# A hybrid decoder block with a top-4-of-32 expert layer: row sums moved into the routing, filler products on TensorE, and a last pair with finer loads, reordered sums and a norm spread over three engines

## The chip, the cores and the metric

The kernel runs on one core of one Trainium2 chip. The metric is the device time of one execution in microseconds (us); of several executions of a kernel the median counts. TensorE is called PE (its weight loads PEld), VectorE DVE, ScalarE ACT, GpSimd POOL, and the queue of SyncE that issues the loads SPq.

## What is computed

One decoder block for 256 tokens of 1024 channels: two token mixers (mLSTM and retention) merged by gates, and then the part that takes three quarters of the time, a layer of 32 experts of which each token uses four. Cut to what matters here:

```python
x = x + gate_m * mixer(h, ...)                       # 256 x 1024
h = rmsnorm(x, norm_ffn_g) * (1.0 + scale_f) + shift_f
logits = h @ w_router + b_router                     # 256 x 32
top_val, top_idx = lax.top_k(logits, 4); top_w = softmax(top_val)
gu = xb @ w_gate_up[e] + b_gate_up[e]                # per expert: 1024 x 2048
y  = clamped_swiglu(gu) @ w_down[e] + b_down[e]      # per expert: 1024 x 1024
x = x + gate_f * sum over the four experts of top_w * y
return rmsnorm(x, norm_final_g)
```

All weights are float32: 12.6 MB for an expert, 403 MB for the 32.

## The kernel before

**Routing.** After the output projection `wout` of the mixer, the residual `x` is transposed (`x1T`), multiplied with the router's weights (`logits`), normalised by one factor per token (`rc`, from a square root on ACT at L63), and the four largest logits give the mask. Three small products (`pos`) number each expert's tokens. The vector `gf` (the gate of the layer, 1024 values) is kept as partial sums on 128 partitions; `row_sum` (L219, L220) makes a row of it that stands on every partition by a product with `ones` and a copy on ACT. Its two halves are summed in pair 0, in the blocks n = 1 and 2.

**Pairs.** Two experts form a pair; there are 16 pairs, one after the other, each with 64 token slots for either expert. For a pair, `gather` builds a 0/1 matrix `oh` and multiplies it with `x` (`xgp`, L1115, eight 128-column products to a `step`); ACT and DVE scale the result into `xg`. Then come six blocks of products: four of `gup` (L1239, gate and up, n = 0 to 3) and two of `dnp` (L1277, down). Each block starts with two small bias products (L224) and runs k = 0 to 7 over the weights of the block, which come as two tiles `a` (k below 4) and `b` of 2 MB each. A product in float32 stands as two records in the profile, so a tile's eight products are "x16". After a `gup` block DVE and ACT make the clamped SwiGLU, and PE transposes it (`aTp`) into `aT`. After a `dnp` block DVE weights the result with the slot's weight and `gf` (`yp`, L1284), ACT and DVE split it in a high and a low part (`yph`, `ypl`), and four products `ya` (L1300) add it to the tokens' sums `yacc`.

**Order.** From the last part of `wout` on, PE runs its instructions in the order in which the code is written. Small work that belongs to the block just finished (the transposes, `ya`) is put in a list `waiting`, and `fill()` empties it within the products of the next block, after k = 4 of a `gup` and k = 3 of a `dnp`. SPq issues every load in the order of the code; a load waits until its buffer's former products are done, and until the eighth load before it has landed.

**The last pair (pair 15).** Its last block is cut into pieces of 256, 128 and 128 columns (`TAIL`), whose weights come in eight loads of 0.5 MB (`taila`, `tailb`). Here `ya` of the block before is not left to the next block: a `fill()` stands right behind it. Each piece is weighted (`yp`) and multiplied back to the tokens (`y`, L1290) at once. `finish` is called for four column ranges, `FIN = (0, 512, 768, 896)`. For each it adds the result to the residual (L1166), squares and sums it (L1168), multiplies by the final norm's row `gn` (L1172), all on DVE. After the last range, the sum gives the norm's factor, ACT and DVE scale the output (L1183 to L1185) and SPq stores it:

```python
                yp = tmp.tile([128, 512], F32, name=f"yp{pair}{n}{c0}", tag="yp", bufs=1)[:, :c1 - c0]
                dve.scalar_tensor_tensor(yp, p[:, :c1 - c0], wsl, gf[:, cs], op0=OP.mult, op1=OP.mult)
                if todo:
                    finish(*todo.pop())
```

Of the kernel before, what the change touches and what calls it, by code (L numbers as in the profile page):

```python
# [10 lines left out]
F32 = mybir.dt.float32  # L11
# [9 lines left out]
D = 1024  # L21
# [91 lines left out]
def block(ctx, tc, I, out, dbg=None):  # L113
# [11 lines left out]
    def f32v(ap):  # L125
        return ap.bitcast(F32)
# [100 lines left out]
    with ExitStack() as mctx:  # L227
# [768 lines left out]
        part = 0  # L996
        for z in range(2):
            w = wslot(wb(z), f"wout{z}", dim=1 + z)
            for c0, c1 in ((0, 256), (256, 512)) if z else ((0, 512),):
# [13 lines left out]
                for i in range(0, 2 * nk, 4):  # L1013
                    tk = [(j // nk, k0 + j % nk) for j in range(i, i + 4)]
                    p = tr(f"x1T{part}{i}")
                    for j, (t, k) in enumerate(tk):
                        pe.transpose(p[:, j * 128:(j + 1) * 128], x[:, t, k * 128:(k + 1) * 128], ident)
                    xt = sb(m2, [128, 4, 128], f"xt{part}{i}", tag="x1T", bufs=2)
                    act.activation(xt.rearrange("p k j -> p (k j)"), p, AF.Copy)
                    for j, (t, k) in enumerate(tk):  # L1020
                        pe.matmul(lp[:, t * E:(t + 1) * E], xt[:, j], wrs[:, k],
                                  start=k == 0 and t == 0, stop=k == 7, skip_group_check=True)
                if part == 1:
                    act.activation(warm, ss[:, 0, 0:1], AF.Sqrt)
                    dve.tensor_add(ss[:, 0], ss[:, 0], ss[:, 1])
# [24 lines left out]
        pe.matmul(pp[:, E:2 * E], tri[:, 1], mask[:, 0], start=False, stop=True)  # L1050

# [106 lines left out]
    o, todo = [], []  # L1158

    def finish(base, c0, c1, src):  # L1160
# [6 lines left out]
        for t in range(2):  # L1167
            dve.scalar_tensor_tensor(o[t][:, cs], x2[:, t, cs], 1.0, x2[:, t, cs], op0=OP.mult, op1=OP.mult,  # L1168
                                     accum_out=ss[:, i, t:t + 1])
        if c1 < D:  # L1170
            for t in range(2):
                dve.tensor_mul(o[t][:, cs], x2[:, t, cs], gn[:, cs])  # L1172
            if i:
                dve.tensor_add(ss[:, 0], ss[:, 0], ss[:, i])
            else:
                act.activation(ss[:, 4, 0:1], ss[:, 0, 0:1], AF.Sqrt)
            return
# [15 lines left out]
    def block_of(src, name):  # L1193
        tiles = [home(f"{name}{h}") for h in "ab"]
        for h in range(2):
            sp.dma_start(tiles[h], src[h])
        return Pairs(tiles)
# [4 lines left out]
    def dn(pair, n):  # L1202
        return block_of(I["w2"][pair, n], f"dn{pair}{n}")
# [4 lines left out]
    def fill():  # L1208

        while waiting:  # L1210
            waiting.pop(0)()
# [5 lines left out]
    for pair in range(NP):  # L1217
# [14 lines left out]
        for n in range(4):  # L1232
# [4 lines left out]
            for k in range(8):  # L1237
# [5 lines left out]
                if k == 4:  # L1243
                    fill()
                    if pair == 0 and n in (1, 2):
                        row_sum(gf, n - 1)
# [12 lines left out]
        for n in range(2):  # L1259
# [10 lines left out]
            for c0, c1 in cuts:  # L1270
# [12 lines left out]
                yp = tmp.tile([128, 512], F32, name=f"yp{pair}{n}{c0}", tag="yp", bufs=1)[:, :c1 - c0]  # L1283
                dve.scalar_tensor_tensor(yp, p[:, :c1 - c0], wsl, gf[:, cs], op0=OP.mult, op1=OP.mult)  # L1284
                if todo:
                    finish(*todo.pop())
                if last and n:
                    y2 = tr(f"y2{c0}").rearrange("p (t c) -> p t c", t=2)
                    for t in range(2):
                        pe.matmul(y2[:, t, :c1 - c0], f32v(ohT[:, t * 128:(t + 1) * 128]), yp, start=True, stop=True)  # L1290
                    todo.append((x2, 512 + c0, 512 + c1, [y2[:, t, :c1 - c0] for t in range(2)]))
                    continue
# [11 lines left out]
                if last:  # L1304
                    fill()
                    todo.append((x, 0, 512, [yacc[t][0] for t in range(2)]))
# [6 lines left out]
    finish(*todo.pop())  # L1313
# [161 lines left out]
```

## Time and profile before

| | |
|---|---|
| median of 3 runs | 1254.34 us (1252.33 to 1255.28) |
| the profiled execution's own time | 1252.83 us |
| its span, first to last instruction | 1251.0 us (1.83 us lie around it) |
| PE busy | 1172.1 us (94%) |
| DVE, ACT, POOL busy | 490.9, 289.4, 3.9 us |
| loaded from HBM | 476.46 MB, mean 382 GB/s |
| mean granted TensorE clock | 0.992 of full speed |

The profile is of one execution. "Busy" counts instructions that run; a busy PE need not be at its peak. The chain that ended last is followed back from the last instruction, at each step to what released it. Where the profile is asked for stretches, a row gives the stretch, its length, the busy time (and count) of PE, PEld, DVE, ACT and POOL, the granted TensorE clock as a share of full speed (1.00 is 2.4 GHz, 0.50 is 1.2 GHz), the share of time in which the 16 DMA engines moved data (it can read a little over 1), and the GB/s moved.

### The profile page before, as it was taken

To read this page: it belongs to the slowest core of one execution; us is meant where nothing else is said; L and a number is where in the kernel's file an instruction comes from. 1 tells how busy PE (TensorE), PEld (TensorE's weight loads), DVE (VectorE), ACT (ScalarE), POOL (GpSimd) and SP (SyncE) were. 2 spreads that over 40 slices of the span, in tenths; PEclk is the share of its full clock that TensorE was granted. 3 is DMA by queue.
4 is the path that set the end of the run, shared out by engine and by line. 5 is a ranking of instruction groups with operands and counts; after the bars stand their busy time and mean duration, and the time that the engine had idled before them with its cause. 6 is when DMAs were issued, how large, how long until landed. Compare 5 with 4: busy or idle time off the path is not lost.

```text
span 1251.0 us, 14561 instructions
## 1 busy us (share of the span) xinstructions
PE 1172.1 (94%) x5872; PEld 582.7 (47%) x5873; DVE 490.9 (39%) x1167; ACT 289.4 (23%) x559; POOL 3.9 (0%) x14
## 2 busy tenths in 40 slices
PE   8999999999899999999998989898989898998985
PEld 6878888888534334343342324232333333232423
DVE  5599889878322222221222222121213122222124
ACT  4585555565211111111110101010101101010111
POOL 0000000000000000000000000000000000000000
PEclk9999999999899999999999999999999999999998
DMA  9956779948899999999999999999999999999993
GB/s 362 366 184 212 292 275 359 353 185 333 318 425 428 427 428 426 429 426 428 427 428 427 427 427 429 428 426 427 428 429 427 427 427 427 430 427 427 427 422 117
DMA packets 43518, 479.12 MB, mean 383 GB/s; under 512 B 5554, under 2 KB 6514, under 8 KB 12212
## 3 DMA queue, kind: packets, MB, share of 16 engines
q1 hardware_dynamic: 42580, 477.53, 92.2%
q8 instruction: 48, 0.79, 0.3%
q10 hardware_dynamic: 864, 0.59, 0.2%
q14 instruction: 26, 0.21, 0.0%
HBM read 476.46 MB, written 1.05 MB: 382 GB/s over the span
## 4 chain that ended last, share of the span: by engine, by line
DMA 54%; PE 42%; DVE 2%; ACT 1%; issue 0%; SPq 0%; ACTq 0%; DVEq 0%
PE gup L1239 10%; PE dnp L1277 5%; DMA gu142b<-in_w 3%; DMA gu102b<-in_w 3%; DMA gu62b<-in_w 3%; DMA gu90b<-in_w 3%; DMA gu130b<-in_w 3%; DMA dn150b<-in_w 3%; DMA gu110b<-in_w 3%; DMA dn90b<-in_w 3%; DMA gu150b<-in_w 3%; DMA dn130b<-in_w 3%; DMA gu82b<-in_w 3%; DMA gu70b<-in_w 3%; DMA dn50b<-in_w 3%; DMA gu122b<-in_w 3%
## 5 line engine op out<-in xcount | busy, mean ns | idle before, releaser
L1151 DVE TENSOR_SCALAR g<-gup 128x256 f32<-128x256 f32 x64 | 27.2, 425 | 345.9 <-PE gup L1239 345.9
L1228 ACT ACTIVATE aT<-aTp 128x256 f32<-128x256 f32 x64 | 24.6, 384 | 286.1 <-PE aTp L1227 286.1
L1115 PEld LDWEIGHTS xgp<-oh,x 128*128 128x128 f32 x512 | 63.5, 195 | 51.4 <-issue 26.0
L1152 ACT ACTIVATE sg<-g 128x256 f32<-128x256 f32 x64 | 26.6, 416 | 255.0 <-DVE g L1151 251.9
L1121 DVE TENSOR_SCALAR xg<-xgp,fsc,fsh 128x128 f32<-128x128 f32 x64 | 26.2, 409 | 146.0 <-ACT xg L1123 146.0
L1115 PE MATMUL xgp<-oh,x 128*128 128x128 f32 x512 | 75.6, 292 | 1.0 <-DVE oh L1107 1.0
L1284 DVE SCALAR_TENSOR_TENSOR yp<-dnp,wsl,gf 128x512 f32<-128x512 f32 (+2 forms) x34 | 24.5, 720 | 114.7 <-PE dnp L1277 112.9
L1123 ACT ACTIVATE xg<-xgp,fsh,fsc 128x128 f32<-128x128 f32 x64 | 29.0, 454 | 153.5 <-PE xgp L1115 153.5
L1294 ACT ACTIVATE yph<-yp 128x512 fp32r<-128x512 f32 x31 | 19.5, 630 | 94.3 <-DVE yp L1284 94.3
L1227 PEld LDWEIGHTS aTp<-ca,a 128*128 128x128 f32 x128 | 13.7, 142 | 39.4 <-issue 39.4
L1155 DVE TENSOR_TENSOR a<-a,sg 128x256 f32<-128x256 f32 x64 | 27.2, 425 | 7.5 <-ACT sg L1152 1.0
L1300 PE MATMUL ya<-yph,ohT 128*128 128x512 f32 x62 | 27.8, 449 | 1.5 <-ACT yph L1294 1.5
L1154 DVE SCALAR_TENSOR_TENSOR a<-a,g 128x256 f32<-128x256 f32 x64 | 27.2, 425 | 2.1
L1227 PE MATMUL aTp<-ca,a 128*128 128x128 f32 x128 | 27.4, 296 | 0.0
L1153 DVE TENSOR_SCALAR a<-gup 128x256 f32<-128x256 f32 x64 | 26.6, 416 | 0.0
L1141 DVE TENSOR_SCALAR ohT<-cwp 128x256 fp32r<-128x256 f32 x16 | 6.8, 425 | 49.3 <-PE cwp L1140 49.3
L1295 DVE TENSOR_TENSOR ypl<-yp,yph 128x512 fp32r<-128x512 f32 x31 | 21.4, 689 | 11.9 <-ACT yph L1294 11.9
L224 PE MATMUL gup<-bex,id 96*64 96x512 bf16 x128 | 25.3, 390 | 0.0
L1300 PE MATMUL ya<-ypl,ohT 128*128 128x512 f32 x62 | 24.5, 396 | 0.2 <-DVE ypl L1295 0.2
L1300 PEld LDWEIGHTS ya<-yph,ohT 128*128 128x128 f32 x62 | 11.6, 187 | 28.1 <-issue 24.3
L224 PEld LDWEIGHTS <-id 96*64 96x64 bf16 x196 | 11.5, 109 | 25.7 <-issue 22.9
L1107 DVE TENSOR_SCALAR oh<-ca,posm,rc 128x64 f32<-128x64 f32 x64 | 17.0, 309 | 6.7 <-PE xgp L1115 6.7
(896 smaller groups left out, 2312.7 us busy)
## 6 DMA issues: line engine op xcount, KB each, us to landing
gu00a<-in_w SPq DMA_DIRECT2D x1, 2048.0 KB, 9.3
gu00b<-in_w SPq DMA_DIRECT2D x1, 2048.0 KB, 7.7
gu01a<-in_w SPq DMA_DIRECT2D x1, 2048.0 KB
gu01b<-in_w SPq DMA_DIRECT2D x1, 2048.0 KB, 7.7
gu02a<-in_w SPq DMA_DIRECT2D x1, 2048.0 KB
gu02b<-in_w SPq DMA_DIRECT2D x1, 2048.0 KB, 13.6
gu03a<-in_w SPq DMA_DIRECT2D x1, 2048.0 KB
gu03b<-in_w SPq DMA_DIRECT2D x1, 2048.0 KB
```

The lines of the kernel that those rows point to most:

```text
L224: pe.matmul(p[rows, :c1 - c0], id3[:, e:e + 1].to_broadcast([96, CAP]), bex[:, n, c0:c1], start=True, stop=False, skip_group_check=True)
L1115: pe.matmul(p[:, q * 128:(q + 1) * 128], x[:, t, k * 128:(k + 1) * 128], oh[:, t].rearrange("p q s -> p (q s)"), start=t == 0, stop=t == 1)
L1123: act.activation(xg[:, k], pq, AF.Identity, bias=fsh[:, k:k + 1], scale=fsc[:, k:k + 1])
L1151: dve.tensor_scalar(g[:r], v[:, 0], LIMIT, None, op0=OP.min)
L1152: act.activation(sg[:r], g[:r], AF.Sigmoid, scale=ALPHA)
L1153: dve.tensor_scalar(a[:r], v[:, 1], LIMIT, -LIMIT, op0=OP.min, op1=OP.max)
L1154: dve.scalar_tensor_tensor(a[:r], a[:r], 1.0, g[:r], op0=OP.add, op1=OP.mult)
L1155: dve.tensor_mul(a[:r], a[:r], sg[:r])
L1227: pe.transpose(p[:, q * 128:(q + 1) * 128], a[:, q * 128:(q + 1) * 128], ident)
L1239: pe.matmul(p[q * CAP:(q + 1) * CAP], xg[:, k, q * CAP:(q + 1) * CAP], w[q, k, slice(0, 512)], start=False, stop=k == 7, skip_group_check= ...
L1277: pe.matmul(p[q * CAP:(q + 1) * CAP, :c1 - c0], aT[:, k, q * CAP:(q + 1) * CAP], w[q, k, slice(c0, c1)], start=False, stop=k == 7, skip_gr ...
L1300: pe.matmul(yacc[t][n], ohT[:, t * 128:(t + 1) * 128], part, start=pair == i == 0, stop=i == 1 and pair >= NP - 2, skip_group_check=True)
```

## The change

There are four edits.

1. The row sums of `gf` leave pair 0. They are made in four quarters of 256 columns (`gate_sum`) in the routing: the first between the last transposes and the last `logits` products, three behind those `logits`. They take two PSUM buffers of the tag `mm`.
2. Five 128-column products of `ones` with itself (`idle`) stand behind the `pos` products. Nothing reads their result.
3. The two 2 MB loads `dn150a`, `dn150b` of the last pair's first `dnp` block become four of 1 MB, of two values of k each.
4. In the last pair, `ya` and the products `y` of each piece wait for the middle of the next piece's products, as elsewhere in the kernel. `finish` now squares and sums on ACT, except one of the two sums of the last range, and multiplies by `gn` on POOL for the first two ranges.

```diff
+        def gate_sum(i):
+            if i == 0:
+                gsum[:] = [mm(f"gsum{h}") for h in range(2)]
+            p = gsum[i // 2][:, i % 2 * 256:(i % 2 + 1) * 256]
+            pe.matmul(p, ones, gf[:, i * 256:(i + 1) * 256], start=True, stop=True)
+            act.activation(gf[:, i * 256:(i + 1) * 256], p, AF.Copy)
...
                     act.activation(xt.rearrange("p k j -> p (k j)"), p, AF.Copy)
+                    if part == 2:
+                        gate_sum(0)
                     for j, (t, k) in enumerate(tk):
                         pe.matmul(lp[:, t * E:(t + 1) * E], xt[:, j], wrs[:, k], ...)
+                if part == 2:
+                    for i in range(1, 4):
+                        gate_sum(i)
...
+        idle = tr("idle")
+        for _ in range(5):
+            pe.matmul(idle[:, :128], ones, ones, start=True, stop=True)
...
-        for t in range(2):
-            dve.scalar_tensor_tensor(o[t][:, cs], x2[:, t, cs], 1.0, x2[:, t, cs], op0=OP.mult, op1=OP.mult,
-                                     accum_out=ss[:, i, t:t + 1])
+        if c1 == D:
+            dve.scalar_tensor_tensor(o[0][:, cs], x2[:, 0, cs], 1.0, x2[:, 0, cs], op0=OP.mult, op1=OP.mult,
+                                     accum_out=ss[:, i, 0:1])
+        for t in range(c1 == D, 2):
+            act.activation(o[t][:, cs], x2[:, t, cs], AF.Square, accum_out=ss[:, i, t:t + 1])
         if c1 < D:
             for t in range(2):
-                dve.tensor_mul(o[t][:, cs], x2[:, t, cs], gn[:, cs])
+                (pool if c0 <= 512 else dve).tensor_mul(o[t][:, cs], x2[:, t, cs], gn[:, cs])
...
-    def block_of(src, name):
+    def block_of(src, name, step=2048):
         tiles = [home(f"{name}{h}") for h in "ab"]
         for h in range(2):
-            sp.dma_start(tiles[h], src[h])
+            for c in range(0, 2048, step):
+                cut = lambda ap: ap.rearrange("p (q c) -> p q c", q=2)[:, :, c:c + step] if step < 2048 else ap
+                sp.dma_start(cut(tiles[h]), cut(src[h]))
...
-        return block_of(I["w2"][pair, n], f"dn{pair}{n}")
+        return block_of(I["w2"][pair, n], f"dn{pair}{n}", 1024 if pair == NP - 1 else 2048)
...
                 if k == 4:
                     fill()
-                    if pair == 0 and n in (1, 2):
-                        row_sum(gf, n - 1)
...
-                if todo:
-                    finish(*todo.pop())
                 if last and n:
-                    y2 = tr(f"y2{c0}").rearrange("p (t c) -> p t c", t=2)
-                    for t in range(2):
-                        pe.matmul(y2[:, t, :c1 - c0], f32v(ohT[:, t * 128:(t + 1) * 128]), yp, start=True, stop=True)
-                    todo.append((x2, 512 + c0, 512 + c1, [y2[:, t, :c1 - c0] for t in range(2)]))
+                    def ended(c0, c1, yp, ohT):
+                        y2 = tr(f"y2{c0}").rearrange("p (t c) -> p t c", t=2)
+                        for t in range(2):
+                            pe.matmul(y2[:, t, :c1 - c0], f32v(ohT[:, t * 128:(t + 1) * 128]), yp, start=True, stop=True)
+                        finish(x2, 512 + c0, 512 + c1, [y2[:, t, :c1 - c0] for t in range(2)])
+                    waiting.append(lambda c0=c0, c1=c1, yp=yp, ohT=ohT: ended(c0, c1, yp, ohT))
                     continue
...
                 if last:
-                    fill()
-                    todo.append((x, 0, 512, [yacc[t][0] for t in range(2)]))
+                    waiting.append(lambda: finish(x, 0, 512, [yacc[t][0] for t in range(2)]))
...
-    finish(*todo.pop())
+    fill()
```

On PE in the last pair, from the end of the first `dnp` block on (`dnp` the product block, `ya` and `y` the products back to the tokens), it stood before:

```order
L1277 MATMUL dnp_6925<-dn150b,aT_6793 64x512 x8
L1300 MATMUL ya_2899<-yph_6950,ohT_6799 128x512
L1300 MATMUL ya_2899<-ypl_6951,ohT_6799 128x512
L1300 MATMUL ya_2901<-yph_6950,ohT_6799 128x512
L1300 MATMUL ya_2901<-ypl_6951,ohT_6799 128x512
...
L1277 MATMUL dnp_6968<-taila,aT_6793 64x256 x16
L1290 MATMUL y_6997<-yp_6987,ohT_6799 128x256 x2
...
L1277 MATMUL dnp_7000<-tailb,aT_6793 64x128 x16
L1290 MATMUL y_7028<-yp_7019,ohT_6799 128x128 x2
```

On PE at the same place of the changed kernel (whose line numbers differ):

```order
L1298 MATMUL dnp_6937<-dn150b,aT_6803 64x512 x8
...
L1298 MATMUL dnp_6976<-taila,aT_6803 64x256 x8
L1323 MATMUL ya_2915<-yph_6962,ohT_6809 128x512
L1323 MATMUL ya_2915<-ypl_6963,ohT_6809 128x512
L1323 MATMUL ya_2917<-yph_6962,ohT_6809 128x512
L1323 MATMUL ya_2917<-ypl_6963,ohT_6809 128x512
L1298 MATMUL dnp_6976<-taila,aT_6803 64x256 x8
...
L1298 MATMUL dnp_7009<-tailb,aT_6803 64x128 x8
L1311 MATMUL y_7020<-yp_7007,ohT_6809 128x256 x2
L1298 MATMUL dnp_7009<-tailb,aT_6803 64x128 x8
```

Each group of products back to the tokens now has half a block of products ahead of it that doesn't need it.

On DVE, the changed kernel's rows from the second piece on (`yp` the weighting, `end` the residual, `ss` the sums of squares, `o` and `end` also the output):

```order
L1305 SCALAR_TENSOR_TENSOR yp_7038<-dnp_7009,wsl_6810,gf 128x128
L1194 TENSOR_TENSOR ss<-ss 128x2
L1184 TENSOR_TENSOR end<-end,y_7051 128x128 x2
L1192 TENSOR_TENSOR o_6991<-end 128x128
L1192 TENSOR_TENSOR end<-end 128x128
L1194 TENSOR_TENSOR ss<-ss 128x2
L1305 SCALAR_TENSOR_TENSOR yp_7069<-dnp_7040,wsl_6810,gf 128x128
```

The last `yp` stands behind two products and a sum that wait for ACT's squares of the range before.

On ACT, the changed kernel's routing (`xt` the transposed residual, `gf` the copies of the row sums, `ss` the square root, `wm` the exponentials of the routing weights, `xg` the first gathered tokens):

```order
L1029 ACTIVATE xt_2847<-x1T_2842 128x512
L1005 ACTIVATE gf<-gsum_2849 128x256
L63 ACTIVATE ss<-ss 128x2
L1005 ACTIVATE gf<-gsum_2849 128x256
L1005 ACTIVATE gf<-gsum_2850 128x256
L1098 ACT_TABLE_LOAD
L1098 ACTIVATE wm<-lg,negm 128x32
L1005 ACTIVATE gf<-gsum_2850 128x256
L1098 ACTIVATE wm<-lg,negm 128x32
L1141 ACTIVATE xg_2924<-xgp_2925,fsh,fsc 128x128
```

Before, the square root followed `xt` at once, and the table load the square root; now one copy stands ahead of the square root, and two ahead of the table load.

## Rows read from the trace of the kernel before

**Rows 1.** stretches: engines' busy us (x instructions), PEclk, DMA share, GB/s

```profile
330.00:335.00 5.00, 5.00 (x30) 2.62 (x28) 0.51 (x2) 0.56 (x2) 0.00 (x0) 1.00 0.27 62
...
340.00:345.00 5.00, 4.53 (x20) 1.44 (x16) 2.06 (x7) 1.08 (x3) 0.00 (x0) 1.00 0.99 403
700.00:900.00 200.00, 184.78 (x878) 67.93 (x877) 47.89 (x124) 21.70 (x50) 0.00 (x0) 0.99 1.01 427
```

**Rows 2.** timeline of the load queue SPq: start us, us, what

```profile
319.11 0.42 SPq L1196 DMA_DIRECT2D dn01a<-in_w  x1
333.82 0.33 SPq L1196 DMA_DIRECT2D dn01b<-in_w  x1
```

**Rows 3.** who SPq waited for, 318 to 345 us: total, times, longest

```profile
SPq L1196 <- PE gup L1239: 21.7, 3, 14.2
```

**Rows 4.** chain that ended last, 324 to 376 us: start, us, what

```profile
324.52 3.75 PE xgp L1115 x16
328.27 0.57 PE gup L224 x2
...
330.82 1.09 PE xgp L1115 x8
331.91 1.87 PE gup L1239 x8
...
344.02 1.13 PE rs L219 x2
...
375.21 1.12 PE ya L1300 x4
```

**Rows 5.** timeline of PE: the first gather; [idle before <-releaser]

```profile
324.52 3.75 PE L1115 MATMUL xgp<-oh,x 128*128 128x128 f32 x16 [0.98 <-DVE oh L1107]
```

**Rows 6.** stretches of low PEclk, and the ones before them

```profile
319.00:322.60 3.60, 1.73 (x12) 1.25 (x12) 2.98 (x19) 2.08 (x3) 0.00 (x0) 0.97 0.94 328
322.60:329.10 6.50, 4.82 (x23) 4.09 (x24) 4.25 (x20) 1.45 (x4) 0.00 (x0) 0.50 1.01 431
...
1223.40:1226.90 3.50, 1.77 (x10) 0.95 (x10) 2.13 (x4) 1.91 (x2) 0.00 (x0) 1.00 0.59 241
1226.90:1230.10 3.20, 3.20 (x18) 1.85 (x16) 3.03 (x8) 0.20 (x1) 0.00 (x0) 0.51 0.20 81
```

**Rows 7.** timeline of PE and its weight loads, last pair

```profile
1214.74 3.65 PE L1277 MATMUL dnp<-dn150a,aT 128*64 128x512 f32 x16 [0.51 <-DMA dn150a<-in_w]
...
1219.79 3.65 PE L1277 MATMUL dnp<-dn150b,aT 128*64 128x512 f32 x16 [1.03 <-DMA dn150b<-in_w]
...
1230.31 1.25 PEld L1277 LDWEIGHTS dnp<-taila,aT 128*64 128x64 f32 x12 [0.19 <-issue]
...
1232.61 1.13 PE L1290 MATMUL y<-yp,ohT 128*128 128x256 f32 x4 [0.59 <-DVE yp L1284]
...
1236.21 0.71 PE L1290 MATMUL y<-yp,ohT 128*128 128x128 f32 x4 [0.54 <-DVE yp L1284]
```

**Rows 8.** chain that ended last, last pair: start us, us, what

```profile
1226.88 5.17 PE dnp L1277 x32
...
1237.10 1.78 PE dnp L1277 x32
...
1242.68 0.49 ACT o L1183
```

**Rows 9.** tile tailb: its four issues, and from issue to landing

```profile
L1267 SPq DMA_DIRECT2D tailb<-in_tail x4: 327/328/328, 1205.0 to 1219.7; - x4
...
DMA to landing us min/median/max: 10.0/13.7/17.3
```

**Rows 10.** groups by line: a GpSimd fill, a VectorE product, a ScalarE copy

```profile
L319 POOL MEMSET gf<- 128x1024 f32 x1 | 1.0, 956 | 0.0
...
L1172 DVE TENSOR_TENSOR o<-end 128x512 f32<-128x512 f32 x1 | 0.7, 684 | 0.0
...
L1228 ACT ACTIVATE aT<-aTp 128x256 f32<-128x256 f32 x3 | 1.2, 384 | 14.2 <-PE aTp L1227 14.2
```

More of the change, by code (lines that the diff above doesn't have):

```diff
@@ L996, in block @@
         part = 0
+        gsum = []
+        def gate_sum(i):
[4 more added lines that the diff above has]
+            act.activation(gf[:, i * 256:(i + 1) * 256], p, AF.Copy)
         for z in range(2):
@@ L1155, in swiglu @@
         dve.tensor_mul(a[:r], a[:r], sg[:r])
-    o, todo = [], []
+    o = []
     def finish(base, c0, c1, src):
@@ L1282, in block @@
                         step(k - 4)
-                yp = tmp.tile([128, 512], F32, name=f"yp{pair}{n}{c0}", tag="yp", bufs=1)[:, :c1 - c0]
+                yp = tmp.tile([128, 512], F32, name=f"yp{pair}{n}{c0}", tag=f"yp{'h' if c0 == 256 else ''}", bufs=1)[:, :c1 - c0]
                 dve.scalar_tensor_tensor(yp, p[:, :c1 - c0], wsl, gf[:, cs], op0=OP.mult, op1=OP.mult)
-                if todo:
-                    finish(*todo.pop())
                 if last and n:
-                    y2 = tr(f"y2{c0}").rearrange("p (t c) -> p t c", t=2)
-                    for t in range(2):
-                        pe.matmul(y2[:, t, :c1 - c0], f32v(ohT[:, t * 128:(t + 1) * 128]), yp, start=True, stop=True)
-                    todo.append((x2, 512 + c0, 512 + c1, [y2[:, t, :c1 - c0] for t in range(2)]))
+                    def ended(c0, c1, yp, ohT):
[4 more added lines that the diff above has]
+                    waiting.append(lambda c0=c0, c1=c1, yp=yp, ohT=ohT: ended(c0, c1, yp, ohT))
                     continue
```

## The prediction

> **What bounds the kernel now.** I read the stretches first. From 340 us on the DMA engines are never idle: their share is 0.99 in 340 to 345 and 1.01 at 427 GB/s over 700 to 900 [rows 1]. PE has slack there: it is busy 184.8 of those 200 us. So the expert stage ends when its last byte has come, and what counts is when the stream began to run without a gap, and what follows its end. The last gap is in 330 to 335, share 0.27 [rows 1]. The load queue shows its cause: `dn01a` is issued at 319.11, `dn01b` only at 333.82 [rows 2], after a wait of 14.2 us for a `gup` product [rows 3], the last one on `gu00a`, which in the chain ends at 331.91 + 1.87 = 333.78 [rows 4]. After `dn01b` the stream has no gap. Whatever moves 333.78 moves everything up to the tail by as much; whatever PE saves after that is slack until the last pair.
>
> The reader is to see two more things. PE's granted clock is at half, 0.50 (1.2 GHz), from 322.6 to 329.1, just where PE works towards 333.78, and at 0.51 from 1226.9 to 1230.1; ahead of either fall PE is busy only 1.73 of 3.6 and 1.77 of 3.5 us [rows 6]. And in the tail PE waits for loads and for its own results, each time on the chain [rows 7].
>
> **Row sums.** Taken from pair 0: two sums of about 1.13 us of PE [rows 4] and their copies. I cost this at nothing: the stream hides it, since PE is ahead of it. Without that cover it would be worth 2.3 us. Added in the routing: four quarters, together the same PE time in places where PE is idle, and four copies on ACT. One copy stands ahead of the square root on which the routing waits. The nearest row, a copy of 256 columns, is 0.384 us [rows 10]: I take a delay of 0.4 (between 0, if PE's `logits` end later anyway, and 0.4). The table load and the exponentials come later, behind two copies more; the weights `wm` need them, the first gather doesn't.
>
> **Filler.** Five 128-column products are ten records. At full clock eight such records take 1.09 us [rows 4], so ten take 1.36, in a wait of 0.98 before the first gather [rows 5]: 0.4 late. At half clock, by 3.75 for sixteen, they take 2.34 and are 1.4 late. What they and the sums buy is the clock. At full clock the sixteen gather records take 2.18, not 3.75, and the two bias products some 0.3, not 0.57 [rows 4]: 1.57 + 0.27 = 1.84. Does the clock hold? The sums add about 2.2 us of products to the 1.73 in 319 to 322.6, which fills that stretch; the filler covers the wait behind it. I take it as held. Stage: +0.4 +0.4 -1.84, **1.0 us earlier**; bounds 1.8 earlier (no delay) and 1.8 later (clock falls, 0.4 + 1.4).
>
> **Finer loads.** PE waits 0.51 for `dn150a` and 1.03 for `dn150b` [rows 7]. With 1 MB loads the first halves land some 2.4 us before the second, PE starts behind its bias products and its transposes, and the second halves are there when it reaches them. Both waits go, 1.54. Do small loads slow the stream? The four 0.5 MB loads of `tailb` are issued from 1205.0 to 1219.7, 4.9 apart; third and last land 13.7 and 10.0 later [rows 9], at 1228.5 and 1229.7, or 1.2 us for 0.52 MB, 430 GB/s: no slower than 2 MB loads. I take no cost. The Trainium skill, "DMA: Bandwidth & Descriptors", section Bandwidth, speaks against the edit: it asks for 1 MiB or more a load for three quarters of peak and gives 341 GB/s for 1 MB against 425 for 16 MB. By it, an estimate, the 4.2 MB would take 12.3 us, 2.5 more than at 427. The rows show loads that overlap in a queue of eight, and speak for no cost.
>
> **`ya` in the next piece's products.** Between the end of `dn150b`'s products (1219.79 + 3.65 = 1223.44) and `taila`'s first (1226.88) [rows 7, 8] lie 3.44 us, in which PE waits for `yp`, `yph`, `ypl`. Of them 0.3 for bias and 1.12 for four `ya` [rows 4] stay, now without a wait, since half of `taila`'s products come first: 2.0 saved. Then the clock should not fall at 1226.9: `taila`'s 32 records take 5.17 [rows 8]; where the clock is back, twelve of their weight loads take 1.25 [rows 7], so 32 take 3.33: 1.84 saved. `taila` and `tailb` land in time: the last piece at 1229.7, while PE, 6.5 us ahead of before in its last block, reaches that piece after 1231; the routing shifts both.
>
> **`y` in the next piece's products.** The waits of 0.59 and 0.54 before `y` [rows 7] go: 1.13. For the last `y` nothing is left to hide it.
>
> **The norm.** Off DVE go most squares and products; they lay beside PE's products, save the last. What is late next is the last `yp`: on DVE it now stands behind two products and a sum that wait for ACT's squares. From `y` of the second range that is two additions, a square, two products and a sum; at 0.2 to 0.4 us each, as for short instructions [rows 10], about 1.4, while PE needs 0.9 for its half block, by 1.78 for a whole one [rows 8]: 0.5 late. In the last range ACT's square runs beside DVE's, 0.2 saved. Net 0.3 lost; bounds 0.2 gained (no wait) and 1 lost. POOL's four products (1536 columns) can start when `ya`, an addition and a square are done: 1223.44 - 1.54 + 0.3 + 1.67 + 1.12 = 1225.0, and 1.4 more, less the routing's 1.0: 1225.4. They must end before the scaling, at 1242.68 [rows 8] less the gain, 1235.5: ten us, or 6.6 ns a column. No row shows a product on POOL; the bounds are its fill, 0.93 ns a column, and, as there is no upper row, the room itself. DVE's is 1.34 [rows 10]. I take it as hidden.
>
> **Sum.** Tail: 1.54 + 2.0 + 1.84 + 1.13 - 0.3 = 6.2. With the 1.0 of the routing 7.2. The profiled execution, 1252.83 (span 1251.0 and 1.83 around it), becomes 1245.6. The median of the runs is 1254.34, 1.5 above it, so the median of the change should be about **1247.1**.
>
> **Rivals.**
> - *The clock falls in the routing all the same.* For it: a wait for the mask remains, and the filler starts behind it. Against: the fuller stretch. Stage 1.8 later, so 4.4 in all: 1249.9.
> - *The tail does not gain its clock, or the finer loads slow the end.* For it: every piece still begins with small products. Against: no wait of PE is left ahead of 1226.9. Costs 1.8 to 2.5: 1249.2.
> - *GpSimd ends last* (slower). The scaling of the first 512 columns and the last store wait for its products, which nothing else runs behind. It decides from 6.6 ns a column, takes the whole gain at 17.3 us (11.3 ns), and makes it 0.2% slower from 19.8 us (12.9 ns, nearly ten times DVE): 1256.9 or more. Against it: the fill's 0.93. The Trainium skill, "GPSIMD Engine Reference", section Performance versus the Vector engine, advises against such products on this engine; its 4497 ns for 2048 columns make, as an estimate, 3.4 us for these four, hidden with six to spare. No run here shows one.
> - *The change moves time but saves none*: the routing loses 1.8, the tail's waits turn into waits for loads or for DVE's queue. Within 2.5 us of before, about 1253.
>
> **Chances.** Forecast 0.62 (its own range 1245 to 1249, from the routing's and the norm's bounds and the runs' scatter); clock falls 0.16; tail gains less 0.12; nothing saved 0.06; GpSimd last 0.04. 0.2% is 2.5 us, about what a measurement of this kernel tells from no change. The first three are faster, less a little for scatter: faster 0.89, same 0.07, slower 0.04. The range takes in both faster rivals and the scatter of the runs, 1.5: 1244.0 to 1251.2.
>
> **What would show it.** `dn01b` issued near 332.8, not 333.82, with a clock of 1.00 from 322 on; if it is later than 333.8 the routing's step is wrong. `dn150a` and `dn150b` without a wait on PE; `taila`'s products starting some 0.3 us after `dn150b`'s end; clock 1.00 through the tail; the last `yp` released by DVE's own queue rather than by PE; POOL idle before the scaling. The forecast fails if the stream has a later gap, if the scaling waits for POOL, or if the time from the scaling to the end (1251.0 - 1242.68 = 8.3 us) changes.

## The result, and the profile after

The changed kernel takes 1245.59 us (median of 5 runs, 1244.96 to 1246.9), the kernel before 1253.87 us (5 runs, 1251.72 to 1255.28): a ratio of 0.9938, 95% interval 0.9923 to 0.9952. A second set of runs gave 0.9944 (0.993 to 0.9957). The prediction, 1247.1 us and faster, holds: the median lies 1.5 us below it. The profiled execution takes 1244.96 us, its span 1243.0, 8.0 less than before.

The account uses four marks: the first `x1T` product (the routing begins), the issue of `dn01b`, the landing of `dn150b` (its last byte), and the first scaling of the output (ScalarE on tile `o`, line 1203). "Routing" is below the time from the first mark to the second, "tail" that from the third to the fourth.

| from, to | before, us | after, us | difference |
|---|---|---|---|
| start, first `x1T` product | 318.86 | 318.37 | -0.49 |
| `x1T`, issue of `dn01b` (routing) | 14.96 | 13.01 | -1.95 |
| `dn01b`, landing of `dn150b` (stream) | 885.83 | 885.77 | -0.06 |
| landing, first scaling (tail) | 23.03 | 16.95 | -6.08 |
| first scaling, end of span | 8.3 | 8.9 | +0.6 |
| span | 1251.0 | 1243.0 | -8.0 |

The stretches of the changed kernel answer to [rows 1, 6]; the columns are the same: busy us of each engine, granted clock, DMA share, GB/s.

```profile
319.00:322.60 3.60, 2.81 (x17) 1.96 (x16) 2.84 (x21) 1.96 (x6) 0.00 (x0) 1.00 0.98 337
322.60:329.10 6.50, 6.50 (x48) 4.68 (x48) 4.08 (x17) 2.76 (x6) 0.00 (x0) 1.00 1.00 429
330.00:335.00 5.00, 5.00 (x30) 2.07 (x28) 1.71 (x6) 0.46 (x1) 0.00 (x0) 1.00 0.57 167
...
700.00:900.00 200.00, 182.88 (x876) 67.61 (x876) 48.12 (x125) 21.18 (x48) 0.00 (x0) 1.00 1.01 427
```

The clock stays at 1.00 (2.4 GHz) where it was 0.50. The gap of the stream is still in 330 to 335, share 0.57 in place of 0.27; after it the stream runs at 427 GB/s as before. The chain of the changed kernel in the routing, start, us and what (answers to [rows 4]):

```profile
323.17 1.21 PE idle L1068 x10
324.38 1.95 PE xgp L1133 x16
326.33 0.34 PE gup L224 x2
...
329.47 1.87 PE gup L1262 x8
```

The first gather takes 1.95 us, not 3.75. The last line, on `gu00a`, ends at 331.34, and the load queue issues `dn01b` at 331.38. PE's timeline in the last pair, with [idle before <-releaser], answers to [rows 7]:

```profile
1211.17 3.60 PE L1298 MATMUL dnp<-dn150a,aT 128*64 128x512 f32 x16
...
1215.08 1.94 PE L1298 MATMUL dnp<-dn150b,aT 128*64 128x512 f32 x8
1217.28 1.94 PE L1298 MATMUL dnp<-dn150b,aT 128*64 128x512 f32 x8 [0.27 <-DMA dn150b<-in_w]
...
1230.66 0.71 PE L1311 MATMUL y<-yp,ohT 128*128 128x128 f32 x4 [0.74 <-DVE yp L1305]
```

and the chain from the landing on (answers to [rows 8]):

```profile
1217.28 1.94 PE dnp L1298 x8
1219.22 0.11 PE dnp L224 x2
1219.33 1.73 PE dnp L1298 x16
1221.06 1.36 PE ya L1323 x4
1222.42 1.88 PE dnp L1298 x16
...
1229.26 0.41 ACT o L1189 x2
...
1230.27 0.07 DVE ss L1194
1230.34 0.27 DVE yp L1305
...
1234.10 0.54 ACT o L1203
```

PE goes from `dn150b` into the first products on `taila` after 0.11 us and does `ya` between their halves: two sixteens, 1.73 and 1.88, in place of 5.17. The chain leaves PE only for the norm: the last `yp` stands behind two products and a sum on VectorE, which wait for ScalarE's squares (`o`, line 1189).

### The profile page after: what moved, and what is told of

Its sections match the earlier page's. It is cut to its first block, busy times and chain, and to the rows that moved or that the text cites. A ratio compares the mean times of both kernels' runs of the same rounds, so it can differ in the third digit from the quotient of the medians.

```text
span 1243.0 us, 14607 instructions
## 1 busy us (share of the span) xinstructions
PE 1167.9 (94%) x5886; PEld 581.9 (47%) x5887; DVE 486.9 (39%) x1149; ACT 292.5 (24%) x575; POOL 7.8 (1%) x18
## 3 DMA queue, kind: packets, MB, share of 16 engines
HBM read 476.46 MB, written 1.05 MB: 384 GB/s over the span
## 4 chain that ended last, share of the span: by engine, by line
DMA 54%; PE 43%; DVE 1%; ACT 1%; SPq 0%; issue 0%; ACTq 0%
PE gup L1262 10%; PE dnp L1298 5%; DMA gu83b<-in_w 3%; DMA gu123b<-in_w 3%; DMA gu51b<-in_w 3%; DMA gu131b<-in_w 3%; DMA gu63b<-in_w 3%; DMA gu143b<-in_w 3%; DMA gu103b<-in_w 3%; DMA gu111b<-in_w 3%; DMA dn91b<-in_w 3%; DMA dn111b<-in_w 3%; DMA dn71b<-in_w 3%; DMA gu151b<-in_w 3%; DMA dn131b<-in_w 3%; DMA dn51b<-in_w 3%
## 5 line engine op out<-in xcount | busy, mean ns | idle before, releaser
L1250 PEld LDWEIGHTS aTp<-ca,a 128*128 128x128 f32 x128 | 13.7, 142 | 39.7 <-issue 39.7
```

Of the source, the lines that this page charges most:

```text
L1250: pe.transpose(p[:, q * 128:(q + 1) * 128], a[:, q * 128:(q + 1) * 128], ident)
```

## The experiments

In three of the profiled executions below (the tail's edits alone, no filler, later steps) the mixer stage, which no kernel here touches, lost about 3 to 4 us some 180 us into the span. In the second of them:

```profile
172.00:176.00 4.00, 4.00 (x19) 3.03 (x18) 4.00 (x11) 1.90 (x3) 0.00 (x0) 1.00 0.02 8
...
180.00:184.00 4.00, 2.62 (x14) 1.89 (x13) 4.00 (x7) 2.56 (x5) 0.00 (x0) 1.00 0.95 365
184.00:188.00 4.00, 4.00 (x17) 3.27 (x17) 3.46 (x8) 0.63 (x1) 0.00 (x0) 0.68 0.96 377
```

In 172 to 176 the changed kernel's share is 0.71, here 0.02; PE then idles 1.4 us and the clock falls. This is scatter of single executions; what follows rests therefore on intervals between the marks, and on medians only where they differ by more.

**Routing alone.** The kernel before with the row sums moved and the filler, its tail as it was:

```diff
+                    if part == 2:
+                        gate_sum(0)
...
+                if part == 2:
+                    for i in range(1, 4):
+                        gate_sum(i)
...
+        for _ in range(5):
+            pe.matmul(idle[:, :128], ones, ones, start=True, stop=True)
...
-                    if pair == 0 and n in (1, 2):
-                        row_sum(gf, n - 1)
```

> Edits 1 and 2 alone (row sums and filler in the routing), the last pair as before. Theory: the clock stays at 1.00 through the routing, so the load dn01b is issued about 2.0 us sooner after the last transposes than before (13.0 us after the first x1T product instead of 15.0), the load stream ends that much earlier, and the whole is 2 us faster (ratio 0.9984), with the tail from dn150b's landing to the scaling at 23.0 us as before. Rival: the routing's gain is slack that the stream eats, the whole is the same within 0.5 us.

Measured: 1250.37 us (11 runs) against 1252.01 of the kernel before (18 runs), ratio 0.9985 (0.9976 to 0.9994). Routing 319.06 to 332.08, 13.02 us; tail 1217.97 to 1240.94, 22.97; clock 1.00 in the routing. The first `x1T` to the landing takes 898.91 us, before 900.79: the 1.9 us of the routing reach the end whole, and touch nothing in the tail.

**Tail alone.** The kernel before with the finer loads, the new order of the last pair and its norm, all of the diff from `finish` on but the lines on `row_sum`:

```diff
+        return block_of(I["w2"][pair, n], f"dn{pair}{n}", 1024 if pair == NP - 1 else 2048)
...
+                    waiting.append(lambda c0=c0, c1=c1, yp=yp, ohT=ohT: ended(c0, c1, yp, ohT))
...
+                    waiting.append(lambda: finish(x, 0, 512, [yacc[t][0] for t in range(2)]))
```

> Edits 3 and 4 alone (finer loads, reordered sums, norm over three engines), the routing as before. Theory: from dn150b's landing to the scaling 17.0 us instead of 23.0, the whole 5.5 to 6 us faster (ratio 0.9955); dn01b issued as late after the transposes as before, 15.0 us, with a clock of 0.50 in between. Rival: part of the tail's gain comes from the earlier stream (a clock that is warm for another reason), then it is under 5 us.

Measured: 1248.33 us (6 runs), ratio 0.9967 (0.9955 to 0.998). Tail 1221.94 to 1238.91, 16.97 us; `dn01a` to `dn01b` 14.10 (before 14.71, after 12.76); the first gather takes 3.66 us. The clock fell in the routing here too, but later and for less long than before (0.85, 0.50 and 0.80 in the three stretches of 2 us from 326 on), and the routing took 14.35 us, not the 15.0 expected. The two halves of the change add up: 22.97 and 16.97 are the tails of before and after, to 0.06. By the ratios of the runs the halves are worth 1.9 and 4.1 us, together 6.0, against 7.8 and 7.0 for the whole change in its two sets: less, but within the intervals.

**No filler.** The changed kernel without

```diff
-        idle = tr("idle")
-        for _ in range(5):
-            pe.matmul(idle[:, :128], ones, ones, start=True, stop=True)
```

> The change without the five filler products. Theory A (the filler holds the clock): the clock falls to 0.50 in the first gather, sixteen gather records take 3.7 us instead of 1.95, and the whole is about 1.8 us slower than the change. Theory B (the row sums alone hold it): the clock stays at 1.00, the gather starts some 0.2 us earlier since it no longer stands behind the filler, and the whole equals the change or is 0.2 us faster. I hold B a little likelier.

Measured: 1246.07 us (4 runs), ratio 0.9951 (0.9935 to 0.9966). Its chain in the routing:

```profile
322.56 0.81 PE x1T L1027 x4
...
328.34 2.18 PE xgp L1130 x16
330.52 0.34 PE gup L224 x2
```

From the first `x1T` to the end of the gather 330.52 - 322.56 = 7.96 us; in the changed kernel 326.33 - 318.37 = 7.96. The gather begins 0.23 earlier and takes 0.23 longer. Routing 13.02, clock 1.00: beside the sums the filler is worth nothing.

**Filler only.** The changed kernel with the row sums back in pair 0 (`gate_sum` and its calls taken out):

```diff
                 if k == 4:
                     fill()
+                    if pair == 0 and n in (1, 2):
+                        row_sum(gf, n - 1)
```

> The change with the row sums back in pair 0 (two halves of 512 columns in its blocks 1 and 2), the filler kept. If the sums hold the clock, it falls to 0.50 ahead of the gather, the filler runs at half speed and the gather starts about 1.4 us late: dn01b 15.5 to 16.5 us after the transposes, the whole 2.5 to 3.5 us slower than the change. If the filler alone is enough, the clock stays at 1.00 and the whole equals the change, with the sums' 2.2 us in pair 0 hidden by the load stream.

Measured: 1248.06 us (6 runs), ratio 0.9967 (0.9955 to 0.9979). Stretches and chain:

```profile
319.00:322.60 3.60, 1.58 (x12) 1.19 (x11) 2.97 (x21) 2.21 (x4) 0.00 (x0) 0.89 1.01 323
322.60:329.10 6.50, 5.96 (x31) 5.78 (x32) 3.80 (x18) 0.98 (x4) 0.00 (x0) 0.54 1.00 426
```

```profile
323.39 2.32 PE idle L1053 x10
325.71 3.24 PE xgp L1118 x16
```

PE is busy 1.58 of 3.6 us ahead of the fall, and the filler then runs at half clock, 2.32 us, in front of the gather. `dn01a` to `dn01b` takes 15.04 us, 2.3 more than with the sums. Over the fourteen profiles of this study: in the three without the sums in the routing (before, this one, tail alone) the clock fell there, in the eleven with them it did not.

**Whole loads.** The changed kernel with `dn` of the last pair in 2048 columns:

```diff
-        return block_of(I["w2"][pair, n], f"dn{pair}{n}", 1024 if pair == NP - 1 else 2048)
+        return block_of(I["w2"][pair, n], f"dn{pair}{n}")
```

> The changed kernel, except that the four transfers of the last pair's `dn` blocks are whole again (2048 columns in one piece, as before the change). Time from the landing of dn150b to the first scaling (16.95 us in the changed kernel). Theory A (the prediction's: the finer loads let the first products of a half begin before the whole half has landed, and the stream pays nothing for them): 18.2 us, that is 0.51 + 1.03 - the 0.27 us that the second half still waited, and a landing that is not earlier; about 1.3 us slower than the changed kernel. Rival B (the Trainium skill's DMA page, that small transfers cost the queue): the landing comes up to 2.5 us earlier counted from dn01b's issue (885.8 us in the changed kernel), and the kernel is not slower.

Measured: 1246.3 us (4 runs), ratio 0.9956 (0.9939 to 0.9972). Its chain:

```profile
1177.98 39.09 DMA dn150b<-in_w
...
1217.21 3.65 PE dnp L1298 x16
...
1231.33 0.29 DVE o L1192
1231.63 0.35 DVE yp L1305
...
1235.46 0.54 ACT o L1203
```

Tail 1235.46 - 1217.07 = 18.39, 1.44 more. Up to the end of `taila`'s products it is 1.72 more (eight products, x16, after the landing, not four); 0.28 comes back at the last `yp`. It still waits for ScalarE's squares, but here VectorE has one product (`o`, 0.29 us) ahead of it, where the changed kernel has two products and a sum (0.65). The code for VectorE is the same in both; of the engines here only PE and the load queue are held to the order of the code. Theory A, 0.2 larger than expected. On the stream: from `dn01b`'s issue, 331.60, to the landing 885.47 us, with finer loads 885.77. Over all profiles it is 885.5 to 885.9 in the four with whole loads (885.8 on average) and 885.3 to 886.9 in the ten with finer ones (886.1). Rival B gets 0.3 on average, less than the scatter, and not 2.5.

**`ya` at once.** The changed kernel with `ya` of the last pair's first half straight behind its `yp`:

```diff
                 if last:
+                    fill()
                     waiting.append(lambda: finish(x, 0, 512, [yacc[t][0] for t in range(2)]))
```

> The changed kernel, except that the products `ya` of the last pair's first half are issued straight behind their `yp` and not within the next block's products. Theory A (PE then waits for VectorE and ScalarE at that place): 2.0 us more from the landing of dn150b to the first scaling, 18.9 to 19.0 us, at a granted clock of 1.00. Rival B (the wait also lets the clock fall in the products behind it): 3.9 us more, 20.8 us, with a stretch below 0.9. Rival C (nothing: the wait lies under the landing of the last loads): 16.9 us.

Measured: 1247.71 us (10 runs), ratio 0.9964 (0.9954 to 0.9974). Tail 1237.25 - 1218.77 = 18.48, 1.53 more, clock 1.00. The chain shows the wait that the change had taken out of it:

```profile
1220.89 0.76 DVE yp L1305
...
1221.67 0.64 ACT yph L1317
...
1223.08 0.97 PE ya L1323 x3
1224.05 0.23 PE dnp L224 x2
1224.28 3.46 PE dnp L1298 x32
```

Up to the end of the 32 records it costs 1.8, less the 0.3 at the last `yp`, where VectorE's order is again that of the run with whole loads. That is theory A's mechanism, 0.4 below its range. The clock did not fall, although PE idled 1.51 and 0.23 us before and between the `ya`. The next run puts both waits back.

**Whole loads and `ya` at once.** The two diffs above together.

> The changed kernel with both edits undone that were undone one at a time: the last pair's `dn` loads whole, and its `ya` products straight behind their `yp`. Each alone left the granted clock at 1.00. Theory A (the clock falls only when both waits stand on PE, so its 1.84 us of the prediction belong to the two edits together): from the landing of dn150b to the first scaling 16.95 + 1.72 + 1.81 - 0.29 + 1.56 = 21.8 us, with a granted clock near 0.5 for some 3 us in the first products of the last block, whose 32 records then take about 5.2 us. Theory B (the clock is held by something else, such as the `y` products or the loads after): 20.2 us at a clock of 1.00, 32 records in 3.5 us.

Measured: 1249.02 us (10 runs), ratio 0.9968 (0.9956 to 0.998). Tail 1237.58 - 1217.38 = 20.20. In the chain:

```profile
1217.52 3.67 PE dnp L1298 x16
...
1223.40 0.97 PE ya L1323 x3
...
1224.60 3.46 PE dnp L1298 x32
```

Theory B to the digit, and mine (A) falls. From the landing to the first product on `taila` PE does the same as before the change, with the same idle times: 0.14, then 3.67 of products, then `ya` to 7.22 us after the landing here, 7.23 before. Before, the 32 records then took 5.17 at a clock of 0.51 [rows 6, 8]; here 3.46 at 1.00. The fall before does not stand alone. The profile of the routing alone, whose tail is the old one, shows it again, at a clock of 0.54:

```profile
1225.31 5.00 PE dnp L1293 x32
```

What differs between those two and this run is the order of `y` and the norm, which VectorE does there (busy 3.03 of the 3.2 us of low clock [rows 6]) and ScalarE and GpSimd here. No run puts these back together with both waits, so neither is shown to be the cause. Chance between executions is a rival as well: each kernel has one profile, and the median of the eleven runs of the routing alone, 1250.37, lies 1.34 us below the one that was profiled, about what the fall costs.

**`y` at once.** The changed kernel with the products `y` of each range straight behind its `yp`:

```diff
                     waiting.append(lambda c0=c0, c1=c1, yp=yp, ohT=ohT: ended(c0, c1, yp, ohT))
+                    fill()
                     continue
```

> The changed kernel, except that the products `y` of each range of the last block are issued straight behind their `yp`, and not within the next range's products. Theory A (PE then waits 0.59 and 0.54 us for `yp`, as before the change, and the last `yp` gets back 0.29 us that it waits for the norm): 17.8 us from the landing of dn150b to the first scaling, in place of 16.95. Rival B (the chain runs over VectorE and ScalarE there anyway): 16.7 to 17.0 us. Rival C (the waits also lower the clock): above 18.5 us, with a stretch below 0.9.

Measured: 1246.66 us (7 runs), ratio 0.9951 (0.9935 to 0.9967). Tail 1234.85 - 1217.06 = 17.79: theory A, 17.8. PE waits 0.59 and 0.46 us before the first two `y`, and 0.46 in place of 0.74 before the last.

**The norm on VectorE.** The changed kernel with all squares and products on VectorE, the order as it is:

```diff
-        if c1 == D:
...
-        for t in range(c1 == D, 2):
-            act.activation(o[t][:, cs], x2[:, t, cs], AF.Square, accum_out=ss[:, i, t:t + 1])
+        for t in range(2):
+            dve.scalar_tensor_tensor(o[t][:, cs], x2[:, t, cs], 1.0, x2[:, t, cs], op0=OP.mult, op1=OP.mult,
+                                     accum_out=ss[:, i, t:t + 1])
...
-                (pool if c0 <= 512 else dve).tensor_mul(o[t][:, cs], x2[:, t, cs], gn[:, cs])
+                dve.tensor_mul(o[t][:, cs], x2[:, t, cs], gn[:, cs])
```

> The changed kernel, except that the squares and the products with the final weight are all on VectorE again, in the changed kernel's order. Theory A (VectorE has no room for them between the row sums of two ranges, since each `yp` stands behind the norm of the range before): from the landing of dn150b to the first scaling 19 to 20 us in place of 16.95: 4.3 us of adds, squares and products of the first half stand ahead of the first `yp` of the last block, which is then 1.8 us late, and about 1 us more is added by the two ranges behind it. Rival B (the order alone brings the gain, the engines do not matter): 16.9 to 17.3 us. Also: VectorE's short sum `ss<-ss` that took 0.40 us beside GpSimd's product in the changed kernel takes 0.15 us here if GpSimd was the cause, and 0.40 us if not.

Measured: 1247.15 us (5 runs), ratio 0.9965 (0.9951 to 0.9979). Tail 1235.95 - 1217.46 = 18.49, 1.54 more: theory A's mechanism, its size 0.5 too large. The norm of the first half stands whole in front of a `yp`:

```profile
1222.30 1.28 DVE end L1184 x2
1223.59 0.61 DVE o L1186 x2
...
1224.81 0.60 DVE o L1190
...
1226.02 0.40 DVE yp L1303
```

That is 3.7 us, not 4.3, and `yp` begins 8.56 us after the landing, in the changed kernel (1224.35) 7.20.

**The last `yp` first.** The changed kernel without the filler, the third range's products on GpSimd, its sum in the last `finish`; and, beside it, the changed kernel again.

```diff
+        if c1 == D:
+            dve.tensor_add(ss[:, 2], ss[:, 0], ss[:, 2])
...
-                (pool if c0 <= 512 else dve).tensor_mul(o[t][:, cs], x2[:, t, cs], gn[:, cs])
-            if i:
-                dve.tensor_add(ss[:, 0], ss[:, 0], ss[:, i])
-            else:
+                pool.tensor_mul(o[t][:, cs], x2[:, t, cs], gn[:, cs])
+            if i == 1:
+                dve.tensor_add(ss[:, 0], ss[:, 0], ss[:, 1])
+            elif i == 0:
...
-        dve.tensor_add(ss[:, 2], ss[:, 0], ss[:, 3])
+        dve.tensor_add(ss[:, 2], ss[:, 2], ss[:, 3])
```

> The changed kernel itself once more, for a direct comparison with the two below. Expected: 1245 to 1247 us, ratio to the kernel before 0.993 to 0.996; from the landing of dn150b to the first scaling 16.9 to 17.0 us.

> The changed kernel without the five filler products, with the products of the third range (128 columns) on GpSimd too, and with that range's sum into `ss` behind the last `yp` on VectorE. Theory A (the last `yp` was 0.3 us late behind two products and a sum that wait for ScalarE's squares; the runs with whole loads and with `ya` at once got those 0.3 us back): landing of dn150b to the first scaling 16.6 to 16.7 us in place of 16.95; x1T to the issue of dn01b unchanged at 13.0 us. Rival B (GpSimd's products of the third range now end too late, or the sum moved is on the chain in its new place): 16.9 us or more. The time of the kernel differs from the changed kernel's by less than the runs' scatter in either case.

Measured: 1245.86 us (5 runs), ratio 0.9944, tail 1234.52 - 1217.56 = 16.96 for the change again; 1246.58 us (5 runs), ratio 0.9953 (0.994 to 0.9967), tail 1233.83 - 1217.01 = 16.82 for the new kernel, between the two theories. VectorE's order still put the moved sum, which waits for the third range's squares, ahead of the last `yp`:

```profile
1229.52 0.30 ACT end L1188 x2
...
1229.84 0.22 DVE ss L1181
1230.07 0.27 DVE yp L1304
```

So 0.13 of the 0.3 came back; the edit did not do all that it was meant to. The sum takes 0.22 us here, not 0.15, because a product on GpSimd runs beside it (see the last section).

**Later steps.** The kernel above with both gather steps behind the fourth k of the first block:

```diff
-                if pair == n == 0 and k in (1, 3):
-                    step(2 + k // 2)
+                if pair == n == 0 and k == 3:
+                    step(2)
+                    step(3)
```

> As the kernel above, and both late gather steps of pair 0 stand behind the fourth k of its first block (now one behind the second and one behind the fourth), so that the last product on gu00a comes 1.09 us earlier. Theory A (the issue of dn01b alone is what the stream waits for): x1T to dn01b 11.9 us in place of 13.0, and x1T to the landing of dn150b 1.1 us shorter than the 898.8 us of the changed kernel. Theory B (the load behind it, which waits for the last product on gu00b, is the next bound): dn01b 1.1 us earlier, but x1T to the landing only 0 to 0.3 us shorter.

Measured: 1246.03 us (5 runs), ratio 0.9941 (0.9927 to 0.9954). `x1T` at 321.38, `dn01b` at 333.15: routing 11.77, 1.24 less. Landing at 1219.16, 897.78 after `x1T`; 898.54 in the kernel above, 898.78 in the changed one. Against these two 0.8 and 1.0 of the 1.24 arrive. The ten profiles with a routing of 13.0 us have 898.3 to 899.9, 899.0 on average; against that it arrives whole, 1.2. Two stretches show the gap ahead of `dn01b` and a second, smaller one (`gu10a` is issued at 338.71):

```profile
332.00:334.00 2.00, 2.00 (x14) 1.10 (x11) 0.00 (x0) 0.00 (x0) 0.00 (x0) 1.00 0.42 172
...
340.00:342.00 2.00, 2.00 (x12) 0.71 (x10) 0.43 (x1) 0.92 (x2) 0.00 (x0) 1.00 0.89 295
```

The kernel above, whose `x1T` lies 2.9 us earlier, has the second gap too: 336 GB/s in 338 to 340. The difference to 295 is about 0.2 us of the stream (an estimate from 41 GB/s over 2 us at 427). The time from `dn01b` to the landing varies by more than the difference between A and B (885.3 to 886.9), so how much the second gap takes isn't settled; theory A fits better. The medians of the three last kernels cannot be told apart.

## Why the prediction was right, point by point

**The bound.** Right. `dn01b` to the landing takes 885.83 and 885.77 us. Single executions scatter from 885.3 to 886.9, but the averages do not depend on the routing: 886.0 in the three profiles in which it took 14.4 to 15.3 us, 886.0 in the ten with 13.0. What the routing saves arrives whole. The three are also the ones with the sums in pair 0, so taking them from there gained the stream nothing, as forecast.

**Row sums, filler, clock.** Right in direction, mis-sized: the stage's 1.0 measured 1.95. The step that was off is the delay of 0.4 + 0.4. The copy ahead of the square root takes 0.38 us but puts it off by 0.13 only (it begins 0.76 us after the copy to `xt` begins, before 0.63); VectorE's work on the one-hot tile began 0.12 late (5.10 us after `x1T`, before 4.98). The filler adds 0.23, so the gather began 0.35 late in all. The gains were 1.80 for the gather (1.57 forecast), 0.23 for the bias and 0.26 for the first `gup` products, which the sum had left out since their clock was back only partly. 0.35 - 1.80 - 0.23 - 0.26 = -1.94. And the reason was half wrong: the filler, which I took to cover the wait, does nothing; with the sums alone the clock holds, with the filler alone it falls.

**Finer loads.** Right: no cost for the stream that stands out of the scatter (0.3 us on average). The term of 1.54 measured 1.74 between the landing and the end of `dn150b`'s products; what counts is how many products are left after the last byte, not the two waits, and one of these did not go whole (0.27 is left before `dn150b`'s second half). The Trainium skill, "DMA: Bandwidth & Descriptors", section Bandwidth, would have had the 1 MB loads cost 2.5 us (an estimate); the runs do not bear that out.

One reading behind "no cost" was wrong [rows 9]. The trace holds the landings of two `tailb` loads only, the second (issued at 1209.8) at 1227.2 and the fourth at 1229.7; 13.7 is the mean of the two, not the third load's. That makes 2.5 us for two loads, 1.05 MB, or 420 GB/s between landings: the same conclusion, by luck. The bytes themselves flow at 241 GB/s by then, with a share of 0.59 [rows 6]. In the prediction's step on `ya`, 6.5 us ahead of 1237.10 is 1230.6, not after 1231; the loads were in time all the same, and PE waits for none behind `dn150b`.

**`ya` and the clock.** `ya`: 2.0 forecast, 1.95 measured (3.42 less 1.47). The clock: 1.84 forecast, 5.17 - 3.61 = 1.56 measured; 32 records take 3.46 to 3.61 at full clock, not 3.33. Its cause, that the waits of PE ahead of 1226.9 lower the clock, is not shown: with both waits back the clock held. What made it fall before stays open, and so does how many executions had the fall. This gain came as forecast, but not for a reason that the runs bear out.

**`y` and the norm.** From the end of `taila`'s products to the last `yp` 6.85 us became 6.04: 0.81 saved, where 1.13 - 0.5 was forecast. The run with `y` at once gives 0.84 net, by its waits 1.05 before the first two `y` less 0.28 at the last: near 1.13 for `y`, and 0.3 for the late `yp`, not 0.5. Those 0.3 hang on VectorE's order (see the run with whole loads). ScalarE's square beside VectorE's saved nothing in the last range (2.65 before, 2.72 after, from `y` to the scaling; 0.2 forecast). Tail: 1.74 + 1.95 + 1.56 + 0.81 + 0.02 = 6.08, forecast 6.2. That the sums are so close is in part luck: 0.20 too little for the loads stands against 0.28 too much for the clock.

**GpSimd last.** The rival did not come about, as weighed: the four products take 3.9 us, 2.5 ns a column, against a room of 6.6; the estimate set beside it was 3.4 us. Its last product ends at 1228.79, 5.3 us ahead of the scaling:

```profile
1224.76 1.26 POOL L1192 TENSOR_TENSOR end<-end 128x512 f32<-128x512 f32 x1
...
1228.06 0.73 POOL L1192 TENSOR_TENSOR end<-end 128x256 f32<-128x256 f32 x1
```

**The total.** 7.2 us forecast for the profiled execution; routing and tail gave 8.03, 0.49 lay ahead of the routing, and 0.6 was lost behind the scaling. The prediction named a change behind the scaling as a way to fail. It and the 0.49 are scatter: `x1T` lies at 318.4 to 319.1 in the executions without the loss in the mixer, and the twelve profiles of the experiments, the one with the old tail among them (9.1), have 8.3 to 9.4 from the scaling to the end. The forecast's median stood on three runs of the kernel before with 1254.34; later sets gave 1252.0 to 1252.9, and 1253.87 over five. That, with the routing's 0.95, is why 1247.1 came out 1.5 high.

## What to carry to other kernels

In a kernel bound by a stream of loads, find the last gap of the stream and the one product that frees the buffer for the load behind it: a microsecond ahead of that product arrives at the end whole, and work that was behind it can lie in idle places ahead of it for little (0.12 us here). After the last byte, count the products that are left rather than the waits: halve the last loads, and put products that wait for another engine between the halves of the next block. An order that takes results later needs free engines as well: with the norm left on VectorE, a quarter of the tail's gain (1.54 of 6.08) was gone.

## What the runs showed of the hardware

- The same products and the same idle times on PE were followed by a clock of 0.51 in the kernel before and of 1.00 with both edits undone. One kernel's executions differ in their mean clock as well: 0.987 to 0.996 over the kernel before. A gain that rests on the clock needs more than one profile.
- A short sum on VectorE waited for a product on GpSimd to end. `ss<-ss`, two columns, took 396 ns beside such a product and 152 later (timelines of POOL and DVE, then the group); with GpSimd idle (the norm on VectorE) both took 152, the last row:

```profile
1227.37 0.73 POOL L1192 TENSOR_TENSOR o<-end 128x256 f32<-128x256 f32 x1 [1.36 <-ACT o L1189]
1227.73 0.40 DVE L1194 TENSOR_TENSOR ss<-ss 128x2 f32<-128x2 f32 x1
```

```profile
L1194 DVE TENSOR_TENSOR ss<-ss x2: 152/274/396, 1227.7 to 1230.2; 128x2 f32<-128x2 f32 x2
```

```profile
L1192 DVE TENSOR_TENSOR ss<-ss x2: 152/152/153, 1229.7 to 1232.1; 128x2 f32<-128x2 f32 x2
```

  The sum ends within 0.02 us of the product's end, and so it does in each of the eleven profiles with products on GpSimd (391 to 396 ns). In the two kernels with the third range's products there too, a sum that began beside a product of 128 columns took 224 ns and ended as closely behind it. So it is a wait of the length that the product has left, not a slower sum. In the changed kernel it costs nothing, since the chain does not pass there; in "The last `yp` first" it does, for 0.07 us. Not every instruction waits: a `yp` of 256 columns, which reads PSUM, took 0.48 us across the end of one such product and the start of the next, with GpSimd idle 0.47.
- GpSimd's product of 512 columns takes 1.26 us, of 256 0.73 and of 128 0.45, against VectorE's 0.684 for 512 [rows 10].
